# Turning groups in pieces of 1024, one last load, and a first store that waits for the second group

## Chip, cores and metric

The kernel runs on one core of one Trainium2 chip. The metric is the device time of one execution in microseconds (us), lower is better. Each execution also has a span, from the first to the last instruction of the program; the device time is longer than the span.

## The reference

```python
def setup_inputs():
    batch, c, h, w = 32, 3, 256, 256
    return {"x": np.random.randn(batch, c, h, w).astype(np.float32)}

def reference(x):
    return np.rot90(x, k=2, axes=(-2, -1)).astype(np.float32)
```

A rotation by 180 degrees reverses each of the 96 images of 65,536 floats as a flat row. 25.17 MB are read and 25.17 MB written; there is no arithmetic.

## The kernel before

Each image is cut into 4 quarters of E = 16,384 floats, one to a partition; 32 images fill the 128 partitions as one group. The three groups A, B and C stay in on-chip memory (SBUF) whole. VectorE reverses each quarter in place, exchanging a piece at the left with one at the right through a small buffer T, and the store writes the four quarters in reverse order.

```python
    E = L // 4
    J = E // 8                                   # pieces of 2048
    ...
    def inside(t):
        for lo in range(0, E // 2, J):
            hi = E - lo - J
            copy(T[:, :], back(t, hi, hi + J))   # back(): read with step -1
            copy(t[:, hi:hi + J], back(t, lo, lo + J))
            copy(t[:, lo:lo + J], T[:, :])

    TAIL = 1536
    load(A, 0, 0, E)
    load(Bt, 1, 0, E)
    body = load(Ct, 2, 0, E - TAIL)
    load(Ct, 2, E - TAIL, E)
    inside(A)
    first = store(A, 0)
    tc.add_manual_dep(first.ins, body.ins.name, ...)   # "queued while the last strip is on its way"
    for g, t in ((1, Bt), (2, Ct)):
        inside(t)
        store(t, g)
```

All loads and stores go through one queue of the sync engine (SP). Each transfer is spread over the 16 DMA engines, 8 rows of 64 KiB to an engine.

## Time and profile before

| | before |
|---|---|
| device time, median of the first 3 runs | 122.15 us (122.03 to 122.24) |
| span of the profiled run | 120.2 us |
| VectorE busy | 44.2 us, 36 copies |
| DMA packets | 1008, share of the engines' span 97.3% |
| one 64 KiB row on one engine | 2.42 us (packet records) |

How to read it: the DMA engines are full from 1.8 to about 119 us and set the time; VectorE works beside them. What counts is any idle moment of a DMA engine.

### The profile page before, as it was taken

How to read it: one execution, taken by the hardware profiler on the slowest of the kernel's cores; microseconds unless marked ns; L12 is line 12 of the kernel's file. 1: busy time of each engine (PE TensorE's matmuls, PEld its weight loads, DVE VectorE, ACT ScalarE, POOL GpSimd, SP SyncE). 2: the span in 40 equal slices, each digit the busy share in tenths (PEclk: the TensorE clock that was granted, in tenths of full speed). 3: DMA queues.
4: the chain of work that ended last, by engine and by line, in shares of the span. 5: the costliest groups of instructions: out<-in, count | busy, mean ns of one | idle time of the engine just before them, and what ended most of it. 6: DMA issues, size and time to landing. Idle time of an engine off the chain costs nothing.

```text
span 120.2 us, 93 instructions
## 1 busy us (share of the span) xinstructions
DVE 44.2 (37%) x36; POOL 0.2 (0%) x4
## 2 busy tenths in 40 slices
DVE  0000000499995099999059999400000000000000
POOL 0000000000000000000000000000000000000000
DMA  9888988898889779779499888988898889888990
GB/s 349 349 349 371 676 349 349 371 676 349 349 349 698 316 316 632 316 336 613 202 408 698 349 349 349 698 349 349 349 698 349 349 349 698 349 349 349 632 414 0
DMA packets 1008, 50.33 MB, mean 419 GB/s; under 512 B 112, under 2 KB 112, under 8 KB 240
## 3 DMA queue, kind: packets, MB, share of 16 engines
q1 hardware_dynamic: 1008, 50.33, 97.3%
HBM read 25.17 MB, written 25.17 MB: 419 GB/s over the span
## 4 chain that ended last, share of the span: by engine, by line
DMA 34%; DVE 25%; another core or an unknown queue 4%; issue 1%; SPq 0%; DVEq 0%
DMA Bt<-in_x_dram 34%; DVE T L52 8%; DVE Bt L52 8%; DVE Ct L52 8%; SPq L55 0%; DVEq L52 0%
## 5 line engine op out<-in xcount | busy, mean ns | idle before, releaser
L52 DVE COPY T<-A 128x2048 f32<-128x2048 f32 x4 | 4.9, 1227 | 22.6 <-DMA A<-in_x_dram 22.5
L52 DVE COPY T<-Ct 128x2048 f32<-128x2048 f32 x4 | 4.9, 1227 | 4.5 <-DMA Ct<-in_x_dram 4.4
L52 DVE COPY T<-Bt 128x2048 f32<-128x2048 f32 x4 | 4.9, 1227 | 4.4 <-DMA Bt<-in_x_dram 4.3
L52 DVE COPY Bt<-T 128x2048 f32<-128x2048 f32 x4 | 4.9, 1227 | 0.1
L52 DVE COPY A<-T 128x2048 f32<-128x2048 f32 x4 | 4.9, 1227 | 0.1
L52 DVE COPY Ct<-T 128x2048 f32<-128x2048 f32 x4 | 4.9, 1227 | 0.1
L52 DVE COPY A<-A 128x2048 f32<-128x2048 f32 x4 | 4.9, 1227 | 0.1
L52 DVE COPY Bt<-Bt 128x2048 f32<-128x2048 f32 x4 | 4.9, 1227 | 0.1
L52 DVE COPY Ct<-Ct 128x2048 f32<-128x2048 f32 x4 | 4.9, 1226 | 0.1
L95 POOL MEMSET const-uint8-127<- 128x1 uint8 x1 | 0.1, 102 | 0.0
L95 POOL MEMSET const-bfloat16-1.0<- 128x1 bf16 x1 | 0.1, 101 | 0.0
L95 POOL MEMSET const-float32-0.0<- 128x1 f32 x1 | 0.1, 98 | 0.2 <-issue 0.2
L95 POOL MEMSET const-float32-1.0<- 128x1 f32 x1 | 0.1, 98 | 0.0
## 6 DMA issues: line engine op xcount, KB each, us to landing
Ct<-in_x_dram SPq DMA_DIRECT2D x1, 7424.0 KB, 57.7
Ct<-in_x_dram SPq DMA_DIRECT2D x1, 768.0 KB, 59.2
A<-in_x_dram SPq DMA_DIRECT2D x1, 21.8
Bt<-in_x_dram SPq DMA_DIRECT2D x1, 40.7
out_dram<-A SPq DMA_DIRECT2D x1, 21.3
out_dram<-Bt SPq DMA_DIRECT2D x1, 39.9
out_dram<-Ct SPq DMA_DIRECT2D x1, 42.9
```

Source lines behind the costliest of these rows:

```text
L52: tc.keep_in_program_order(nc.vector.tensor_copy(out=dst, in_=src))
L95: nc = _bacc.Bacc("TRN2", target_bir_lowering=False, num_devices=1)
```

## The change

The intent was one transfer less, and a release of the stores that hangs on VectorE, not on a strip of a load. The pieces are halved, so that the turning of B ends about when the strip's release used to come.

```diff
-    J = E // 8
+    J = E // 16
...
-            copy(t[:, lo:lo + J], T[:, :])
+            last = copy(t[:, lo:lo + J], T[:, :])
+        return last
 
-    TAIL = 1536
     load(A, 0, 0, E)
     load(Bt, 1, 0, E)
-    body = load(Ct, 2, 0, E - TAIL)
-    load(Ct, 2, E - TAIL, E)
+    load(Ct, 2, 0, E)
     inside(A)
+    last = inside(Bt)
     first = store(A, 0)
     tc.add_manual_dep(
-        first.ins, body.ins.name,
+        first.ins, last.ins.name,
         ...)
-    for g, t in ((1, Bt), (2, Ct)):
-        inside(t)
-        store(t, g)
+    store(Bt, 1)
+    inside(Ct)
+    store(Ct, 2)
```

More of the change, by code (lines that the diff above doesn't have):

```diff
@@ L51, in copy @@
     def copy(dst, src):
-        tc.keep_in_program_order(nc.vector.tensor_copy(out=dst, in_=src))
+        return tc.keep_in_program_order(nc.vector.tensor_copy(out=dst, in_=src))
     def load(t, g, lo, hi):
@@ L64, in inside @@
             copy(t[:, hi:hi + J], back(t, lo, lo + J))
-            copy(t[:, lo:lo + J], T[:, :])
-    TAIL = 1536
+            last = copy(t[:, lo:lo + J], T[:, :])
+        return last
     load(A, 0, 0, E)
     load(Bt, 1, 0, E)
-    body = load(Ct, 2, 0, E - TAIL)
-    load(Ct, 2, E - TAIL, E)
+    load(Ct, 2, 0, E)
     inside(A)
+    last = inside(Bt)
     first = store(A, 0)
     tc.add_manual_dep(
-        first.ins, body.ins.name,
+        first.ins, last.ins.name,
         mybir.DependencyInfo(mybir.DependencyClass.Sync, mybir.DependencyReason.DATA),
-        reason="the first store is queued while the last strip is on its way")
-    for g, t in ((1, Bt), (2, Ct)):
-        inside(t)
-        store(t, g)
+        reason="the first store is queued when the second group is turned")
+    store(Bt, 1)
+    inside(Ct)
+    store(Ct, 2)
 _INS = ['x']
```

## The prediction

> **What bounds the kernel now.** I read the page of the profiled execution first: the engines' busy shares, the forty slices, the DMA queue.
>
> ```profile
> span 120.2 us, 93 instructions
> ...
> DVE 44.2 (37%) x36; POOL 0.2 (0%) x4
> ...
> DVE  0000000499995099999059999400000000000000
> POOL 0000000000000000000000000000000000000000
> DMA  9888988898889779779499888988898889888990
> ...
> q1 hardware_dynamic: 1008, 50.33, 97.3%
> ```
>
> The reader is to see that VectorE (DVE) has work only in the middle third, while the 16 DMA engines have work in every slice but the last. One queue moves 25.17 MB in and 25.17 MB out, and its packets fill 97.3% of the 16 engines' span. So the kernel is bound by the DMA engines, and the time can only change if they get an idle gap, lose one, or move bytes at another rate. Each engine moves 6 transfers x 8 rows of 64 KiB; the packet records of the trace give 2.42 us for such a row, so 48 x 2.42 = 116.2 us of pure transfer in a span of 120.2. The other 4.0 us are the start (first packet at 1.78 us), slower first packets (about 3 us each instead of 2.42), the last landing (119.45 us) and the end of the program.
>
> The chain of waits on the page says DMA 34%, DVE 25%. That is the chain through the last store's issue, not what fills the time: the last store is issued at 76.51 us and lands 42.9 us later, because it queues behind two other stores. So I next asked where the DMA engines could run dry. There is one such place, the change from loads to stores. The timeline shows who issues what there.
>
> ```profile
> 55.80 1.23 DVE L52 COPY Bt<-T 128x2048 f32<-128x2048 f32 x1
> 59.48 0.63 SPq L58 DMA_DIRECT2D out_dram<-A  x1
> 60.20 0.55 SPq L58 DMA_DIRECT2D out_dram<-Bt  x1
> 61.38 1.23 DVE L52 COPY T<-Ct 128x2048 f32<-128x2048 f32 x1 [4.35 <-DMA Ct<-in_x_dram]
> ...
> 76.51 0.54 SPq L58 DMA_DIRECT2D out_dram<-Ct  x1
> ```
>
> Group A has been turned since 37.6 us and group B since 57.03; the first store is held until 59.48 us by the landing of the body of the third load (its last semaphore update is at 59.38). The packet records show the handover: store packets start at 60.76 to 60.94 us, 1.28 us after the issue began; the load packets of the 16 engines end between 60.33 and 60.84. The engines thus wait about 0.2 us on average (at most 0.43) for their first store packet. The handover is already nearly seamless, and the store's issue at 59.48 sets it almost exactly. That is the one number the change can move.
>
> **What the Trainium skill says.** "DMA: Bandwidth & Descriptors", section "Where 436 GB/s comes from", gives a port ceiling of 435 GB/s; the trace agrees: 65,536 B in 2.42 us on 16 engines is 433 GB/s, so no faster transfer is left to find. "Perfetto Trace Analysis", section "DMA Instruction — HWDGE (DVE, Sync)", says that the reported window of a DMA instruction is descriptor generation, not data movement; the trace agrees, 0.63 us for a store whose data take 19.3, and the first packet comes 0.65 us after that window ends. "VectorE: DVE Perf Modes", section "The perf-mode tier table", gives 1227 ns for a 2048-element fp32 copy in SBUF and 693 ns for a 2048-element bf16 copy, which takes half as many cycles; the trace has 1227 ns for the first, and reads backwards cost no more than forwards. "Vector Engine (DVE) Microarchitecture Reference", section "5.2 Measured stream behaviour on trn2", gives 1.0417 ns per column at one element a cycle and about 75 ns fixed per instruction after overlap; the slope fits below, the fixed part does not: the starts of successive copies lie 1.261 us apart, which leaves 194 ns over 2048/2 x 1.0417 = 1067 ns.
>
> **The change part by part.**
>
> *The pieces of 1024.* Removes 36 copies of 2048, adds 72 of 1024. This is the row to be halved:
>
> ```profile
> L52 DVE COPY T<-Bt 128x2048 f32<-128x2048 f32 x4 | 4.9, 1227 | 4.4 <-DMA Bt<-in_x_dram 4.3
> L52 DVE COPY Bt<-T 128x2048 f32<-128x2048 f32 x4 | 4.9, 1227 | 0.1
> L52 DVE COPY Bt<-Bt 128x2048 f32<-128x2048 f32 x4 | 4.9, 1227 | 0.1
> ```
>
> One copy is 1067 ns of stream plus 160 ns fixed, and 34 ns pass before the next. With 1024 elements it is 533 + 160 = 693 ns, which is also the skill's 693 for half the cycles; the pitch is 727 ns (an estimate, from the row above and that table). A group has 24 copies instead of 12: 24 x 0.727 = 17.4 us instead of 12 x 1.261 = 15.1 us, so 2.3 us more per group. A load takes 19.4 us per group (22.51 to 41.93), so turning still keeps up: A would run 22.5 to 39.9, before B lands; B 41.93 to 41.93 + 17.45 - 0.03 = 59.35; C, landed at about 61.3, to about 78.8. All of it lies beside transfers. C's end moves from 76.5 to 78.8, but the engines have A's and B's stores queued until about 61 + 2 x 19.35 = 99.6 us, so 20 us of slack remain. What is on the path is only B's end, because of the next part.
>
> *The new wait.* Takes away the wait for the third load's body and puts the end of B's turning in its place. After the last copy of C the sequencer's store began 0.02 us later (76.49 to 76.51), while the semaphore of a load needed 0.10 (59.38 to 59.48). So the first store would be issued at 59.35 + 0.02 = 59.37 us: 0.11 us earlier than now. Its first packets would come at 59.37 + 1.28 = 60.65 us and up. The two old and new release times are as good as equal; that coincidence is the heart of the forecast. The second store waits no longer for its own turning, which is now implied.
>
> *The last load as one transfer.* Removes 128 packets of 6,144 B (234 ns each) and makes the 59,392 B ones (2,194 ns) whole rows (2,420 ns): 8 x (2194 + 234 - 2420) = 64 ns less per engine, plus one semaphore packet of 9 ns. One issue of about 0.5 us on the sync queue goes as well, early and hidden. The loads end about 0.07 us earlier. The landing of C is unchanged otherwise, as all 16 engines served the strip last anyway.
>
> *Sum.* The engines' load work ends at about 60.26 to 60.77 and the store packets come at about 60.65 to 60.83; the whole of the store stream, 3 x 19.35 us, shifts earlier by 0.07 to 0.11 us. 122.15 - 0.1 is 122.05; I predict 122.1 us.
>
> **The rivals.** (1) *Smaller copies are dearer than thought, and the first store comes late.* Each 0.01 us on the pitch puts 0.24 us on B's end, and past 0.809 us (19.42 us a group) A's turning delays B's too and it becomes 0.48. To be 2% slower, the store must come about 2.5 us late, at 62.0 us: 22.51 + 48p = 62.0 gives p = 0.823 us, a fixed part of 290 ns against the 194 measured. For it: the slack is nil, every error shows in full. Against it: two lengths in the skill's table, and this trace for one of them, agree on the fixed part. A pitch of 0.75 would make 122.6 us, one of 0.823 about 124.6. (2) *Copies are cheaper*, with a fixed part of 75 ns: B ends near 56.5, the stores queue behind the last load and the 0.2 us of waiting vanishes: 121.9 us, and no more, as the engines have no other hole. (3) *The strip and its late start of stores were protecting something*, such as loads slowed by stores that begin on some engines while others still read. The slices show no slower packets where the two kinds meet (2.48 us for the first store row against 2.42), so this would be 0.1 us. (4) *Stores hidden anyway*: C's later turning could cost only if it moved by 20 us; it moves by 2.3, so it costs nothing.
>
> **Range and chances.** Up by rival 1's moderate form (pitch 0.75, 0.5 us), down by rival 2 (0.2 us) and by run-to-run spread (122.03 to 122.24): 121.8 to 122.7. Over 2% faster is ruled out by the 433 GB/s, 1%. Over 2% slower needs a pitch 13% above the estimate, or a hitch I don't see: 4%. Within 2%: 95%.
>
> **What would show it.** Right: copies of 1024 at 690 to 700 ns with starts 0.727 us apart; B's last copy ending at 59.2 to 59.5 us and the first store issued right after; no dip of the DMA row in the slices around 60 us beyond now; DMA packets 864 + 96 = 960; C turned near 78.8 with no effect. Wrong: a store issue after 60 us, with an idle stretch of the DMA engines as long as the time lost; or row packets that are no longer 2.42 us.

## More of the kernel before

The DMA issues of the page give the time from a transfer's issue to its landing, that is, to the last engine's completion:

```profile
out_dram<-A SPq DMA_DIRECT2D x1, 21.3
out_dram<-Bt SPq DMA_DIRECT2D x1, 39.9
out_dram<-Ct SPq DMA_DIRECT2D x1, 42.9
```

The first store lands 21.3 us after its issue; keep that number for comparison. The packet records add that the 16 engines end their last rows between 118.90 and 119.11 us, the slowest 0.12 us behind the mean of the other 15.

## The result, and the profile after

The changed kernel takes 122.78 us (median of 6 runs, 122.71 to 122.94) against 122.20 us for the kernel before in the same rounds (122.03 to 122.77). The ratio is 1.0041, 95% interval 1.0019 to 1.0063. Here and below a ratio is the mean time of one kernel's fast runs over that of the other's of the same rounds, so it is not quite the ratio of the medians quoted. The forecast of "within 2%" held, but 122.78 lies just outside the range of 121.8 to 122.7: half a microsecond came from somewhere that the prediction had not counted.

The page of the changed kernel, the lines that answer to those of before:

```profile
span 121.2 us, 126 instructions
...
DVE 50.0 (41%) x72; POOL 0.2 (0%) x4
...
q1 hardware_dynamic: 864, 50.33, 96.7%
q14 instruction: 1, 0.01, 0.0%
...
L52 DVE COPY T<-Bt 128x1024 f32<-128x1024 f32 x8 | 5.6, 694 | 2.2 <-DMA Bt<-in_x_dram 2.0
...
out_dram<-A SPq DMA_DIRECT2D x1, 22.2
out_dram<-Bt SPq DMA_DIRECT2D x1, 40.8
```

In the copy's line, x8 is the count; then come its busy time in us, the mean ns of one copy, and VectorE's idle time before it. The copies take 694 ns, as worked out. (The packets are 864 in all, 6 x 128 rows and 6 x 16 completions; the 960 of the prediction counted the completions twice.) New is the second queue line: one packet of 0.01 MB that fetches *instructions* while the data move. And the first store now lands 22.2 us after its issue instead of 21.3.

The timeline of the sync queue in the same run:

```profile
59.63 0.63 SPq L58 DMA_DIRECT2D out_dram<-A  x1
60.30 0.59 SPq L58 DMA_DIRECT2D out_dram<-Bt  x1
79.04 0.54 SPq L58 DMA_DIRECT2D out_dram<-Ct  x1
```

In this execution the first store is issued 0.15 us later than in the profile before, not 0.11 earlier. That gave two theories:

- **Fetch theory.** VectorE's program of 72 copies is long enough to need another block of instructions. The block is fetched by one of the 16 DMA engines, which is full of data; that engine falls behind, and the slowest engine sets the end.
- **Late-store theory.** The later first store, or another part of the new order of loads and stores, costs the time.

The packet records of the changed kernel show the fetch at close range, in us from the span's start. (They don't name the engine; packets are put to one engine where one starts as another ends. Joined so, the row with the latest end is on the engine that fetched.)

```
  the one engine that fetched          start     took
  row of the first store (64 KiB)      65.850    2.722    (2.42 elsewhere)
  instruction packet (8192 B)          68.569    0.309
  next row                             68.875    2.768    (2.42 elsewhere)
  last row ends: this engine 119.94, the next slowest 119.47, mean of the other fifteen 119.13
```

0.30 + 0.31 + 0.35 us are lost on that engine, and it ends 0.81 us behind the mean of the others (the slowest in the kernel before: 0.12). Most of the rest it makes up later, with rows of 2.418 us against 2.424 on the others. This is suggestive, but one trace is one execution; hence the experiments.

### The profile page after: what moved, and what is told of

It is laid out like the page before. It is cut to its first block, busy times and chain, and to the rows that moved or that the text cites. A ratio compares the mean times of both kernels' runs of the same rounds, so it can differ in the third digit from the quotient of the medians.

```text
span 121.2 us, 126 instructions
## 1 busy us (share of the span) xinstructions
DVE 50.0 (41%) x72; POOL 0.2 (0%) x4
## 4 chain that ended last, share of the span: by engine, by line
DMA 34%; DVE 28%; another core or an unknown queue 2%; issue 1%; SPq 0%; DVEq 0%
DMA Bt<-in_x_dram 34%; DVE T L52 9%; DVE Ct L52 9%; DVE Bt L52 9%; SPq L55 0%; DVEq L52 0%
## 5 line engine op out<-in xcount | busy, mean ns | idle before, releaser
L52 DVE COPY T<-A 128x1024 f32<-128x1024 f32 x8 | 5.6, 694 | 23.0 <-DMA A<-in_x_dram 22.8
L52 DVE COPY T<-Ct 128x1024 f32<-128x1024 f32 x8 | 5.6, 694 | 2.2 <-DMA Ct<-in_x_dram 2.0
L52 DVE COPY T<-Bt 128x1024 f32<-128x1024 f32 x8 | 5.6, 694 | 2.2 <-DMA Bt<-in_x_dram 2.0
L52 DVE COPY A<-A 128x1024 f32<-128x1024 f32 x8 | 5.6, 694 | 0.3
L52 DVE COPY Ct<-Ct 128x1024 f32<-128x1024 f32 x8 | 5.6, 694 | 0.3
L52 DVE COPY Ct<-T 128x1024 f32<-128x1024 f32 x8 | 5.6, 694 | 0.3
L52 DVE COPY Bt<-T 128x1024 f32<-128x1024 f32 x8 | 5.5, 694 | 0.3
L52 DVE COPY Bt<-Bt 128x1024 f32<-128x1024 f32 x8 | 5.5, 694 | 0.3
L52 DVE COPY A<-T 128x1024 f32<-128x1024 f32 x8 | 5.5, 693 | 0.3
## 6 DMA issues: line engine op xcount, KB each, us to landing
out_dram<-A SPq DMA_DIRECT2D x1, 22.2
```

Of the source, the lines that this page charges most:

```text
L52: return tc.keep_in_program_order(nc.vector.tensor_copy(out=dst, in_=src))
```

## The experiments

Twelve kernels ran, beside the kernel before in the same rounds. In the table, span and total are means of the runs, and "late" is how far the slowest engine's last row ends behind the mean of the other fifteen in the profiled run.

| kernel | VectorE copies | instruction packets | late, us | span | before's span | total minus span | ratio (95%) |
|---|---|---|---|---|---|---|---|
| split48 | 48 | 0 | 0.25 | 120.43 | 120.43 | 2.21 | 1.0035 (1.0020 to 1.0050) |
| pad36 | 72 | 1 | 0.85 | 121.50 | 120.43 | 1.79 | 1.0088 (1.0067 to 1.0108) |
| rule_only | 36 | 0 | 0.41 | 120.82 | 120.43 | 1.80 | 1.0032 (1.0014 to 1.0051) |
| pieces_only | 72 | 1 | 0.76 | 121.22 | 120.43 | 1.79 | 1.0068 (1.0053 to 1.0084) |
| after_again | 72 | 1 | 0.77 | 120.98 | 120.48 | 1.80 | 1.0043 (1.0030 to 1.0056) |
| late48 | 50 | 0 | 0.10 | 121.75 | 120.48 | 1.90 | 1.0113 (1.0095 to 1.0130) |
| pad12 | 48 | 0 | 0.13 | 120.40 | 120.48 | 2.20 | 1.0028 (1.0014 to 1.0042) |
| pad24 | 60 | 1 | 0.85 | 121.20 | 120.48 | 1.80 | 1.0061 (1.0047 to 1.0075) |
| act36 | 36 (and 36 on ScalarE) | 0 | 0.20 | 120.40 | 120.40 | 1.79 | 1.0000 (0.9987 to 1.0012) |
| pad164 | 200 | 2 | 1.60 | 122.12 | 120.40 | 1.80 | 1.0142 (1.0128 to 1.0155) |
| early_store | 36 | 0 | 0.50 | 121.30 | 120.40 | 1.76 | 1.0072 (1.0054 to 1.0091) |
| tail1792 | 36 | 0 | 0.44 | 120.60 | 120.40 | 1.78 | 1.0015 (1.0002 to 1.0029) |

### 1. split48: the changed kernel with a shorter program

Only B, whose end releases the first store, stays in pieces of 1024.

```diff
-    J = E // 16                       # all groups
+    J = E // 8                        # A and C
...                                    # inside() gets the piece as an argument
-    last = inside(Bt)
+    last = inside(Bt, E // 16)
```

> Group B stays in pieces of 1024 and the first store still waits for the end of B's turning, as in the changed kernel; A and C go back to pieces of 2048, so VectorE runs 48 copies instead of 72. Fetch theory (72 copies make the program long enough for an 8 KiB instruction fetch at 68.6 us, which one of the full DMA engines serves and which holds that engine back by about 0.8 us): no instruction packet in the trace, all engines end together, 122.0 to 122.2 us. Late-store theory (the first store's issue, 59.63 against 59.48 us, costs the time): the same issue near 59.6 and 122.7 to 122.9 us, as in the changed kernel.

Measured: 122.69 us against 122.24. On the total alone the late-store theory would have won. The span says otherwise:

```profile
span 120.5 us, 102 instructions
...
DVE 46.1 (38%) x48; POOL 0.2 (0%) x4
...
q1 hardware_dynamic: 864, 50.33, 97.1%
...
out_dram<-A SPq DMA_DIRECT2D x1, 21.4
```

There is no instruction packet, the first store lands after 21.4 us again, and the mean span of the runs is 120.43 us, the same as before's. The profiled execution issues its first store at 59.63 us, just as the changed kernel's, and its span is 120.53 against 121.16 us. So one load, the store rule and that issue time don't explain the loss, against the late-store theory. The 0.42 us lie outside the span: total minus span is 2.21 us instead of 1.79. That was not expected by either theory, and pad12 takes it up.

### 2. pad36: the kernel before with a longer program

```diff
+    S = pool.tile([P, 8], x.dtype, tag="S")
...
+    for _ in range(36):
+        copy(S[:, :], T[:, 0:8])      # behind the last turning
```

> The kernel before with 36 copies of 8 elements added on VectorE behind the last turning, so 72 copies as in the changed kernel; loads, stores and waits untouched. Fetch theory: one instruction packet in the trace, near 80 us, one engine's last packets 0.7 to 0.9 us after the others', 122.6 to 122.9 us. Late-store theory: nothing on the path has changed, 122.1 to 122.3 us.

Measured: 123.22 us against 122.24. Nothing that moves data was touched, VectorE's extra work (copies of 172 ns) ends at 84 us, and the mean span is 1.07 us longer (0.95 without one run of 122.1). The page has the packet:

```profile
q1 hardware_dynamic: 1008, 50.33, 96.5%
q14 instruction: 1, 0.01, 0.0%
```

In the packet records it starts at 83.27 us; the row before it took 2.71 us, the row after 2.77, and that engine ends 0.85 us behind the others. Thus a longer VectorE program alone costs this much, in fact more than the whole change does.

### 3. rule_only: the new loads and store rule, pieces of 2048

```diff
-    J = E // 16
+    J = E // 8
```

> The last load in one transfer and the first store after B's turning, but pieces of 2048 (36 copies). B ends at 57.05 us, so the store is queued about 3.5 us before the loads run out. Fetch theory: no instruction packet; the 0.2 us that the engines wait at the handover vanish, 121.9 to 122.1 us. Late-store theory: an issue earlier by 2.4 us should gain at least as much as it lost in the changed kernel, 121.5 to 121.8 us.

Measured: 122.65 us against 122.24, a loss where both theories expected a gain. There is no instruction packet. The timeline and the issues tell what happened:

```profile
57.16 0.62 SPq L58 DMA_DIRECT2D out_dram<-A  x1
57.82 0.59 SPq L58 DMA_DIRECT2D out_dram<-Bt  x1
62.22 1.23 DVE L52 COPY T<-Ct 128x2048 f32<-128x2048 f32 x1 [5.09 <-DMA Ct<-in_x_dram]
```

```profile
Ct<-in_x_dram SPq DMA_DIRECT2D x1, 60.5
out_dram<-A SPq DMA_DIRECT2D x1, 24.4
```

C lands later: VectorE starts on it at 62.22 us instead of 61.38. In the packet records the last load row of the 16 engines took 3.10 us on average instead of 2.42. The stores already stood in the queue behind it. The idle 0.2 us at the handover did vanish, but 0.68 us of slower rows came in its place. So "earlier is better" is false for the first store in this kernel; why the rows are slower is not shown.

### 4. pieces_only: the kernel before, pieces of 1024

```diff
-    J = E // 8
+    J = E // 16
```

> The kernel before with pieces of 1024 and nothing else: the first store still waits for the body of the third load, which lands at 59.4 us; B's turning ends at the same moment. 72 copies. Fetch theory: an instruction packet near 68 us, 122.6 to 122.9 us. Late-store theory: the store is issued at 59.5 as before, 122.1 to 122.3 us.

Measured: 122.99 us against 122.24; span 0.79 us longer. The instruction packet comes at 68.41 us; the engine that fetched ends 0.76 us behind the others. The store issue is the old one:

```profile
59.48 0.63 SPq L58 DMA_DIRECT2D out_dram<-A  x1
```

With that same issue time the profiled span is 121.00 us against 120.23 before. The halved pieces alone bring the loss, and rather more of it than the whole change shows.

### 5. after_again: the changed kernel beside the others

No edit.

> The changed kernel once more, to have it beside the others on one chip. Fetch theory: one instruction packet near 68.5 us, one engine ends 0.5 to 0.9 us after the others, span 120.9 to 121.2 us, 122.7 to 122.9 us. If the fetch were an accident of one execution, the packet would be absent or elsewhere.

Measured: 122.75 us against 122.25, ratio 1.0043, all as in the first comparison. The instruction packet is there again, at 68.30 us. In this execution the second load landed earlier, and the store's timing is the predicted one to the hundredth:

```profile
58.65 0.69 DVE L52 COPY Bt<-T 128x1024 f32<-128x1024 f32 x1
59.37 0.63 SPq L58 DMA_DIRECT2D out_dram<-A  x1
60.05 0.59 SPq L58 DMA_DIRECT2D out_dram<-Bt  x1
```

The store is issued 0.11 us earlier here than in the profile of the kernel before, and the span is still 0.66 us longer (120.89 against 120.23 us): a second argument against the late-store theory. The hundredth is luck. In the first profile of the same kernel the issue came at 59.63, because B landed at 42.07 us and not at 41.81, and that span is 0.27 us longer. So the moment of the handover does pass into the span, but it varies from execution to execution, with the old loads too (59.48 to 59.81 us in the profiles of the kernel before and of the padded ones).

### 6. late48: a store that is really late

split48 with two more copies before the first store.

```diff
+    for _ in range(2):
+        last = copy(T[:, 0:E // 16], T[:, E // 16:E // 8])
     first = store(A, 0)
```

> The kernel of 48 copies (only B in pieces of 1024) with two more copies of 1024 elements on VectorE between the end of B's turning and the first store, so the store is issued 2 x 0.73 = 1.46 us later, at about 61.1 us. If the handover to the stores is on the path, as the prediction has it, the span goes up from 120.43 by 1.3 to 1.5 us, to 121.7 to 121.9. If the end is set elsewhere, it stays at 120.4.

Measured: 123.66 us against 122.25; span 121.75, which is 1.27 us over before's (expected 1.3 to 1.5).

```profile
61.05 0.63 SPq L58 DMA_DIRECT2D out_dram<-A  x1
```

So the handover is on the path, as the prediction had it, and a store 1.4 us late costs nearly all of that. In the two profiles of the changed kernel its issue lies 0.11 us before and 0.15 us after the old one, too little for the loss.

### 7. pad12: is the 0.4 us outside the span the program's length too?

pad36 with 12 small copies instead of 36, so 48 in all, as in split48.

> The kernel before with 12 copies of 8 elements behind the last turning, 48 copies in all. Fetch theory with a trigger between the 48th and the 58th copy: no instruction packet while data move, span as before, 120.4; but the end after the span 0.4 us longer, as in the other kernel of 48 copies, so about 122.65 us. If the 0.4 us there came from the store rule or the one load, the total is 122.2 us.

```profile
DVE 46.1 (38%) x48; POOL 0.2 (0%) x4
...
q1 hardware_dynamic: 1008, 50.33, 97.2%
```

There is no q14 line. Measured: 122.63 us against 122.25; span 120.40 (before 120.48), total minus span 2.20 us. The loads, stores and waits here are those of the kernel before, so the 0.4 us behind the span belong to the program's length (48 copies), not to the change's rule. In the semaphore records of split48 one engine comes 0.41 us later than in the others to the last barrier after the program. That VectorE then waits for the same block of instructions is likely, but no packet of it is recorded; it is argued, not shown. With 50 copies (late48) the surplus is down to 0.1 us, with 60 and more it is gone.

### 8. pad24: on the other side of the threshold

> The same with 24 small copies, 60 in all. Fetch theory: the trigger is passed, so an instruction packet between 79 and 84 us, one engine late by 0.6 to 0.9 us, span 121.0 to 121.5 and total minus span back at 1.8 us: 122.8 to 123.3 us. If only the amount of VectorE work mattered: 122.2 us.

```profile
DVE 48.2 (40%) x60; POOL 0.2 (0%) x4
...
q1 hardware_dynamic: 1008, 50.33, 96.7%
q14 instruction: 1, 0.01, 0.0%
```

Measured: 123.01 us against 122.25; an instruction packet at 83.08 us, one engine 0.85 us behind, span 121.20, total minus span 1.80. Twelve more copies of 172 ns, in the shadow of the stores, add 0.8 us to the span and take away the 0.4 behind it. 50 copies bring no fetch while data move, 60 do. If the fetch was asked for while the engine moved the first slow row, the trigger lies between the 54th and the 58th copy (an estimate: in the changed kernel that row ran from 65.85 to 68.57 us, C's copies start at 61.57 and every 0.728 us, and 48 copies are done before). The same reading of pad24 gives the 55th to the 60th.

### 9. act36: the whole change without the long program

All the change as it is, but A's and half of C's copies on ScalarE, with a buffer of its own.

```diff
...                                    # U, copy_act, and inside() with its arguments
-    inside(A)
+    inside(A, copy=copy_act, T=U)
...
-    inside(Ct)
+    inside(Ct, 0, E // 4)
+    inside(Ct, E // 4, E // 2, copy=copy_act, T=U)
```

> The changed kernel with all its 72 pieces of 1024, its one last load and its store rule, but 36 of the copies (all of A, half of C) on ScalarE with a buffer of its own, so that VectorE and ScalarE run 36 each. The copies on ScalarE may take up to 1.5 us each without touching the end (A has 37 us until the first store, C 40). Theory that the length of one engine's program calls the fetch: no instruction packet while data move, span 120.3 to 120.6, 122.1 to 122.4 us. Theory that the pieces or the total number of copies cost: span 120.9 to 121.2, about 122.8 us.

Measured: 122.17 us against 122.16, ratio 1.0000 (0.9987 to 1.0012).

```profile
DVE 25.0 (21%) x36; ACT 38.9 (32%) x37; POOL 0.2 (0%) x4
...
q1 hardware_dynamic: 864, 50.33, 97.3%
...
L56 ACT COPY U<-A 128x1024 f32<-128x1024 f32 x8 | 8.4, 1045 | 20.8 <-DMA A<-in_x_dram 20.6
```

The same 72 pieces, the same load, the same rule, slower copies (1045 ns), no instruction packet, and no loss. This is the deciding run: what costs is neither the pieces nor the new wait, but how many instructions one engine's program has.

### 10. pad164: two packets

> The kernel before with 164 copies of 8 elements behind the last turning, 200 in all: 128 more than in the run with 36 of them[...]. Fetch theory: at least two instruction packets while data move. If the packets meet one DMA engine, that engine is late by twice as much, span about 122.2; if two engines, the end is set by the later one alone, span 121.2 to 121.6.

Measured: 123.90 us against 122.16; span 1.72 us longer.

```profile
q14 instruction: 2, 0.02, 0.0%
```

The packets start at 83.22 and 110.44 us. One engine ends 1.60 us behind the other fifteen, twice the usual 0.8, and the next slowest only 0.25 us behind their mean. Both packets thus met the same DMA engine, and the cost adds up.

### 11. early_store: a store queued 20 us ahead

rule_only without the wait for B.

> One last load, pieces of 2048, and the first store waits only for A's own turning, so it is queued at about 37.6 us, 20 us before the loads run out, instead of at 57.1 as in the run with the rule alone. Queueing theory (rows of the last load take about 3.1 us instead of 2.42 when a store stands behind them in the queue): the same as there, last load rows near 3.1 us, span 120.7 to 121.0. If it was the issue itself at 57 us that disturbed the loads: those rows at 2.42 us and a span of 120.2 to 120.4.

Measured: 123.03 us against 122.16; span 0.90 us longer, worse than rule_only's 0.39.

```profile
37.72 0.63 SPq L58 DMA_DIRECT2D out_dram<-A  x1
57.11 0.55 SPq L58 DMA_DIRECT2D out_dram<-Bt  x1
```

The last load rows took 3.04 to 3.78 us in the packet records, mean 3.44. The run separates the two theories less cleanly than meant, since B's store is issued at 57.11 us here, where rule_only issues A's. But the load rows under way at 37.72 us, when A's store was issued, took 2.42 us each, and so did the later ones up to 57.3 us with the store standing behind them. In both runs only the last load row, the one directly before a store row, is slow. So an issue alone does not slow the rows, at least not at 37.72; whether the issue near 57 us plays a part, and why the loss is larger here than in rule_only, stays open.

### 12. tail1792: can the handover be closed better?

The kernel before with `TAIL = 1792`, the only try to beat both kernels.

> The kernel before with the strip of the last load widened from 1536 to 1792 elements, so that the first store is issued about 0.3 us earlier and its packets meet the end of the loads without the 0.2 us of idle engines. Handover theory: 0.1 to 0.2 us gained, span 120.2 to 120.4. If a store queued behind the last load rows slows them: nothing gained or up to 0.4 us lost.

Measured: 122.35 us against 122.16, ratio 1.0015 (1.0002 to 1.0029), so at best nothing. In the profiled run the body landed late (59.62 us) and the store was issued at 59.71, no earlier than before, so the run tested its own idea badly and is inconclusive on it. No version was found that beats the kernel before; act36 equals it.

## Why the prediction was wrong by half a microsecond

By its own steps:

- **The bound** was read rightly: full DMA engines, one place where they can run dry. late48 shows that this place is on the path.
- **The copies** were right: 694 ns against 693, starts 0.728 us apart against 0.727, B's end and the store's issue at 59.37 us in after_again (to the hundredth by luck, see there).
- **The new wait** was right in its effect: split48 has the changed kernel's release and before's span.
- **The gain of 0.1 us** from one load and an earlier release did not show: split48 and act36 equal before's span within 0.02 us.
- **The step that failed** is the sentence on the pieces, "All of it lies beside transfers", and with it the sum "122.15 - 0.1 is 122.05". The copies do lie beside the transfers. But 36 more instructions are themselves data that one of the DMA engines must bring, and it does so in line with rows of 2.4 us. The missing term is an 8 KiB instruction packet: the engine that fetches ends about 0.8 us behind the others (0.77 and 0.81 in the two profiles of the changed kernel). The span grew by 0.50 us in after_again. The prediction counted what the instructions do and for how long, not how many there are. Its own signs of being wrong did not warn of this: the first store did not come after 60 us, and of the row packets only the two beside the instruction packet were slowed by it.
- **The rivals.** The first (dearer copies, late store) is refuted for this kernel by the 694 ns. The second, that an earlier release would give 121.9 us, had a wrong consequence: rule_only, with B's end at 57.1 us, took 122.65. The third, that the late start of the stores protects the loads, was set at 0.1 us; it is real, 0.39 us of span in rule_only and 0.90 in early_store, but does not occur in the changed kernel, whose release at 59.4 to 59.6 us comes late enough. The fourth held.
- **The range** had room only for errors of the copies' pitch; "a hitch I don't see" got its chance at over 2% but no width below that.

The Trainium skill has a page on this that the prediction did not use: "Runtime: NRT & Kernel Launch", section "Instruction fetch mechanics", says that an engine's sequencer drives its own DMA queue to fetch the next page while it executes the current one, and calls the cost mostly hidden. The traces agree on the fetch by DMA (one packet in the changed kernel, at 68.57 us), and differ on the cost where the DMA engines are the bound: that engine ends about 0.8 us late.

What stays open: the packet goes with 0.50 us more of span in the changed kernel, 0.72 in pad24, 0.79 in pieces_only and 1.07 in pad36, though the engine that fetches is behind by 0.76 to 0.85 in all of them. The profiles take this apart. In the twelve whose first store does not stand behind running loads, the fifteen engines other than the slowest end, on average, 58.13 to 58.18 us after the mean start of the first store's packets; when the handover comes, the rest follows. These packets start at 60.74 us in after_again, 60.83 in the kernel before and 61.14 in pad36. So pad36's span is longer than before's by 0.31 us of handover, 0.73 of lateness and 0.1 after the last row; after_again's by -0.09, 0.65 and 0.1. Only profiled executions can be read like this, so how much of the differences between the mean spans is the handover's is not shown.

## What to carry to other kernels

Where, as here, full DMA engines set the time, count the instructions of each engine and not only their work: a program that grows too long (here between 50 and 60 VectorE copies) has more instructions fetched by a DMA engine that is full of data, and the slowest engine sets the end; keep the program short, or divide it over two engines. Look for an instruction queue in the profile's DMA lines, and at how long a transfer takes to land, before explaining a few tenths of a microsecond by waits. And a store queued far ahead behind running loads is not free: release it so that its first packet meets the end of the loads.

## What the Trainium skill lacked or had wrong

- "Runtime: NRT & Kernel Launch", "Instruction fetch mechanics": it gives refills of 16 KiB and calls the boundary mostly hidden. Every fetch within the spans here is a packet of 8,192 B, and one goes with 0.50 to 1.07 us more of span when the DMA engines are full, two with 1.72. With 200 copies (pad164) there is a second packet, with 72 (pad36) there is not.
- No page says that a program somewhat shorter than the one that fetches can lose time after its last instruction: total minus span is 2.20 to 2.21 us with 48 VectorE copies, 1.90 with 50, about 1.79 with 36 and 1.80 with 60.
- "DMA: Bandwidth & Descriptors" has nothing on the speed of loads with a store queued behind them on the same engines: the last load rows of 64 KiB took 3.10 us (store queued at 57.2 us) and 3.44 us (at 37.7 us) instead of 2.42.
- "Vector Engine (DVE) Microarchitecture Reference", "5.2 Measured stream behaviour on trn2": about 75 ns fixed per instruction after overlap; dependent fp32 copies here start 1.261 us apart for 2048 elements and 0.728 for 1024, which leaves about 195 ns over the two-a-cycle stream.
